# Two raw and three low-part weight tiles, a new product order, spread convolution tiles

## The chip, the cores and the metric

The kernel runs on one core of a Trainium2 chip. The metric is the device time of one execution in microseconds; the value for a kernel is the median of several executions. Five engines take part: PE (TensorE, matrix products), DVE (VectorE, elementwise work), ACT (ScalarE, activations and copies), POOL (GpSimd) and SP, which here issues nearly all transfers from one queue.

## The reference

One decoder layer runs on two groups of tokens with the same weights: a prompt of 512 tokens and 8 samples of 8 tokens, 576 tokens in all, with a model width of 2048.

```python
c = split_columns(rms_norm(x, ln_g) @ w_in)          # 2048 -> 10312 columns
# attention branch: indexer scores, top-k of keys, softmax, times silu(z_attn), @ w_up_attn
u = c['glu_val'] * sigmoid(c['glu_gate'])
dw = depthwise_conv(u_pad, conv_w) + conv_b          # 31 taps, 1024 channels
conv_out = silu(layer_norm(dw, conv_norm_g, conv_norm_b)) @ w_pw + b_pw
branch_conv = (conv_out * silu(c['z_conv'])) @ w_up_conv
merged = sigmoid(c['gate_attn']) * branch_attn + sigmoid(c['gate_conv']) * branch_conv
y = rms_norm(x + merged @ w_out, final_g)
```

Keys, values, indexer keys and the convolution's last rows are outputs too. All is float32.

## The kernel before

**Products.** Activations lie transposed, channels on partitions and the 576 tokens along the free dimension. Each float32 operand is held as two parts in a reduced format (`fp32r`): a high part, and the low part that is left. A product is three matmuls (high by high, high by low, low by high). `weight_unit` (line 140) loads a raw weight tile of 128 x 8 x 128 (512 KB) into a tile called `wraw` (three buffers); `split` (line 147) has ACT write the high part `whi` (line 151, three buffers) and DVE the low part `wlo` (line 153, two buffers). `block` (line 227) runs 48 matmuls on one such unit, for two halves of the tokens.

**Two ways through the input projection.** The first columns (indexer, keys, values, queries, `z_attn`, six of eight convolution tiles and six of eight `z_conv` tiles) go through `block`. The remaining columns (convolution tiles 6 and 7, the last two `z_conv` tiles, 2 x 16 gate tiles) go through `strassen` (line 156): two column tiles, two halves of the channels and two halves of the tokens form a 2 x 2 product of blocks that takes seven products of 24 matmuls instead of eight. I call one call of it a pair; there are 19. A pair loads four raw tiles b11, b12, b22, b21, makes four sums of them on DVE (t3, b12-b11, t2, b21-t2), splits seven tiles, and combines the seven results by seven additions of 128 x 288 on DVE (line 191). In the order before, the products are A11, S1, S2, A12, S3, S4, A22, where S1 to S4 name sums of activation blocks. `XA` (line 943) says where each activation operand lies.

**Sums of activations.** Ahead of the first pair, lines 919 to 933 form S1, S2 and S4 (tiles `s12`, `s4`) through a temporary `f` with one buffer; lines 933 to 939 then overwrite a quarter of the activations with S3. The temporary `f` lies in a pool that is closed before the pool `p3` is opened, which holds the tiles `wx`, `wt` and `sk` of the pairs; `p3` takes its memory.

**Convolution tiles.** `conv_tile` (line 644) multiplies value and gate, then runs 31 taps on DVE (line 706), a small part for the samples (lines 712, 713), and stores the result. Its `u` and `dw` tiles have two buffers each.

**Layer norm of the convolution.** Lines 983 to 1023 run it in two halves of the tokens, eight tiles each, beside the gate pairs. Line 1019 takes a sigmoid on ACT, line 1020 an affine map on DVE.

**End.** `w_pw`, `w_up_attn`, `w_up_conv` go through `block`; then the output projection `w_out` runs in two passes, the second half of the tokens first (line 1107), with one half per pass, so that a raw tile feeds 24 matmuls only. Its residual rows `y` are loaded on the same SP queue (line 1116).

**Order.** A planner lays out each engine's instructions ahead of time, by priority and by its own estimates of durations. Priorities (the function `pri`): weight loads and splits 0, evictions and additions (`EV`) 1, chains such as the sums and the layer norm (`CH`) 3, the convolution's taps and the top-k (`TK`) 5, matmuls 6; the lowest number that is ready goes first. On the chip each engine keeps that order, whatever the real durations are.

Of the kernel before, what the change touches and what calls it, by code (L numbers as in the profile page):

```python
# [20 lines left out]
SEQ = 512  # L21
# [64 lines left out]
def build(tc, I, O):  # L86
# [52 lines left out]

    def weight_unit(w, width, c0, n, kt0, lvl=0):  # L140

        with pri(lvl) if lvl is not None else nullcontext():
            raw = per.tile([128, 8, 128], F32, name="wraw", tag="wraw", bufs=3)
            dma(raw[:, :, :n], ap(w, kt0 * 128 * width + c0, [[width, 128], [128 * width, 8], [1, n]]))
            return split(raw, n)

    def split(raw, n=128):
# [4 lines left out]
        lo = per.tile([128, 8, 128], R, name="wlo", tag="wlo", bufs=2)[:, :k, :n]  # L152
# [3 lines left out]
    def strassen(pool, w, width, ca, cb, A, ev, kts=16, lvl=6, EV=1):  # L156
# [3 lines left out]
        with pri(0):  # L160
            raws = []
            for c0, half, tag in ((ca, 0, "wx"), (cb, 0, "wraw"), (cb, 1, "wraw"), (ca, 1, "wx")):
                t = (per.tile([128, 8, 128], F32, name="wraw", tag="wraw", bufs=3) if tag == "wraw" else
# [3 lines left out]
            b11, b12, b22, b21 = raws  # L167
            t2 = pool.tile([128, 8, 128], F32, name="t2", tag="wt", bufs=2)[:, :n]
            t3 = pool.tile([128, 8, 128], F32, name="t3", tag="wt", bufs=2)[:, :n]

        def bank():
            return ps.tile([128, 512], F32, name="mms", tag="mm", bufs=4)[:, :T2]
# [14 lines left out]
        k1, k5, u2, u3 = (kept() for _ in range(4))  # L187
# [20 lines left out]
        with pri(EV):  # L208
            ev(0, 0, k1)
        p = product(t3, "S3")  # L210
        add(u3, p, u2)
        add(u2, u2, k5)
        add(k5, u3, k5)
        with pri(EV):
            ev(1, 1, k5)
        p = product(b22, "S4")
        add(u2, p, u2)
        with pri(EV):
            ev(0, 1, u2)
        with pri(0):  # L220
            v.tensor_sub(b21, b21, t2)
        p = product(b21, "A22")
        add(u3, p, u3)
        with pri(EV):
            ev(1, 0, u3)
# [418 lines left out]
    def conv_tile(c, pair=None):  # L644
# [17 lines left out]
        else:  # L662
            held = []

            def ev(i, b, x):
                if b == 0:
                    s.activation(sg[:, TS2[i]], x, AF.Sigmoid)
                if (i, b) == (1, 1):
                    held.append(x)
                if (i, b) == (0, 1):  # L670
                    v.tensor_mul(up[:, 30:30 + T2], x, sg[:, :T2])
                if (i, b) == (1, 0):
# [537 lines left out]
```

## Time and profile before

| quantity | value |
|---|---|
| time, median of 3 runs | 1640.47 us (1639.73 to 1640.93) |
| profiled execution: its time, its span | 1639.57 us, 1637.6 us |
| PE busy | 1588.6 us (97%) |
| PE weight loads (PEld) busy | 1538.3 us (94%) |
| DVE busy | 1115.0 us (68%) |
| ACT busy | 664.0 us (41%) |
| POOL busy | 82.1 us (5%) |
| mean granted TensorE clock | 0.991 |
| transfers | 219.53 MB, mean 134 GB/s |

The page also has the busy share of each engine in 40 slices of some 41 us:

```
PE   7999999999999999898999999999999999999997
DVE  6437884476585989999998999667543343445554
PEclk8999999999999999999999999999999999999998
```

A digit is tenths of the slice. PE is full for most of the span; DVE is full from about 640 to 960 us. Neighbouring instructions on DVE overlap in the records, so that the distance from start to start is shorter than the duration.

### The profile page before, as it was taken

How to read it: one execution, taken by the hardware profiler on the slowest of the kernel's cores; microseconds unless marked ns; L12 is line 12 of the kernel's file. 1: busy time of each engine (PE TensorE's matmuls, PEld its weight loads, DVE VectorE, ACT ScalarE, POOL GpSimd, SP SyncE). 2: the span in 40 equal slices, each digit the busy share in tenths (PEclk: the TensorE clock that was granted, in tenths of full speed). 3: DMA queues.
4: the chain of work that ended last, by engine and by line, in shares of the span. 5: the costliest groups of instructions: out<-in, count | busy, mean ns of one | idle time of the engine just before them, and what ended most of it. 6: DMA issues, size and time to landing. Idle time of an engine off the chain costs nothing.

```text
span 1637.6 us, 28579 instructions
## 1 busy us (share of the span) xinstructions
PE 1588.6 (97%) x11594; PEld 1538.3 (94%) x11594; DVE 1115.0 (68%) x1905; ACT 664.0 (41%) x1089; POOL 82.1 (5%) x97
## 2 busy tenths in 40 slices
PE   7999999999999999898999999999999999999997
PEld 5889999999999999888899999999999999899996
DVE  6437884476585989999998999667543343445554
ACT  5434322264555443243344555445421111444443
POOL 4200000001111100000000000000000000400000
PEclk8999999999999999999999999999999999999998
DMA  6732534344444334323345545443744444464864
GB/s 193 203 87 86 163 109 114 99 132 132 136 129 133 93 86 114 112 73 97 102 127 168 149 121 148 133 132 94 242 126 128 127 121 134 142 167 142 258 179 129
DMA packets 318963, 219.53 MB, mean 134 GB/s; under 512 B 14549, under 2 KB 293205, under 8 KB 318112
## 3 DMA queue, kind: packets, MB, share of 16 engines
q1 hardware_dynamic: 316144, 208.27, 43.9%
q0 software_dynamic: 2688, 9.44, 1.8%
q8 instruction: 91, 1.49, 0.4%
q14 instruction: 40, 0.33, 0.1%
HBM read 188.81 MB, written 32.24 MB: 135 GB/s over the span
## 4 chain that ended last, share of the span: by engine, by line
PE 80%; DVE 12%; DMA 3%; issue 2%; ACT 1%; POOL 1%; POOLq 0%; ACTq 0%; DVEq 0%; SPq 0%
PE mm L237 55%; PE mms L181 15%; DVE wlo L153 3%; PE mm L457 2%; DVE dw L706 2%; DMA wraw<-in_w_out 1%; PE po L786 1%; PE po L855 1%; PE pw L768 1%; DVE sk L191 1%; DMA wraw<-in_w_in 1%; POOL ml L1096 1%; PE pw L782 1%; DVE wraw L198 1%; PE pw L517 1%
## 5 line engine op out<-in xcount | busy, mean ns | idle before, releaser
L237 PE MATMUL mm<-x,whi 128*128 128x256 f32 (+2 forms) x2496 | 452.3, 297 | 0.0
L151 ACT CAST whi<-wraw 128x1024 fp32r<-128x1024 f32 (+1 forms) x228 | 238.5, 1046 | 523.0 <-PE mm L237 386.6
L153 DVE TENSOR_TENSOR wlo<-wraw,whi 128x1024 fp32r<-128x1024 f32 (+1 forms) x228 | 279.0, 1224 | 207.4 <-PE mm L237 116.0
L237 PEld LDWEIGHTS mm<-x,whi 128*128 128x128 f32 (+1 forms) x2496 | 377.9, 187 | 5.7 <-issue 3.8
L237 PE MATMUL mm<-x,wlo 128*128 128x256 f32 (+2 forms) x1248 | 274.7, 297 | 0.0
L181 PE MATMUL mms<-x,whi 128*128 128x288 f32 x1216 | 248.2, 298 | 6.8 <-ACT whi L151 5.9
L237 PEld LDWEIGHTS mm<-x,wlo 128*128 128x128 f32 (+1 forms) x1248 | 209.0, 187 | 0.9 <-issue 0.4
L181 PEld LDWEIGHTS mms<-x,whi 128*128 128x128 f32 x1216 | 197.3, 190 | 8.0 <-ACT whi L151 6.6
L181 PE MATMUL mms<-x,wlo 128*128 128x288 f32 x608 | 182.5, 300 | 7.2 <-DVE wlo L153 6.9
L181 PE MATMUL mms<-s,whi 128*128 128x288 f32 x912 | 186.0, 296 | 0.0
L706 DVE SCALAR_TENSOR_TENSOR dw<-u,cp,dw 128x512 f32<-128x512 f32 x240 | 177.8, 750 | 1.6
L181 PEld LDWEIGHTS mms<-s,whi 128*128 128x128 f32 x912 | 146.6, 188 | 0.5 <-ACT whi L151 0.3
L181 PE MATMUL mms<-s,wlo 128*128 128x288 f32 x456 | 135.9, 298 | 6.2 <-DVE wlo L153 6.1
L181 PEld LDWEIGHTS mms<-x,wlo 128*128 128x128 f32 x608 | 115.7, 190 | 10.9 <-DVE wlo L153 10.6
L237 PE MATMUL mm<-mh,wlo 128*128 128x256 f32 (+1 forms) x416 | 122.7, 300 | 3.0 <-DVE wlo L153 3.0
L237 PE MATMUL mm<-mh,whi 128*128 128x256 f32 (+1 forms) x416 | 122.0, 294 | 1.6 <-ACT whi L151 1.6
L237 PE MATMUL mm<-ml,whi 128*128 128x256 f32 (+1 forms) x416 | 121.5, 294 | 0.0
L181 PEld LDWEIGHTS mms<-s,wlo 128*128 128x128 f32 x456 | 85.7, 188 | 9.4 <-DVE wlo L153 9.2
L151 ACT CAST whi<-wx 128x1024 fp32r<-128x1024 f32 x57 | 59.8, 1050 | 82.4 <-PE mms L181 69.5
L237 PE MATMUL mm<-cT,whi 128*128 128x256 f32 (+1 forms) x512 | 88.9, 295 | 0.0
L237 PE MATMUL mm<-aT,whi 128*128 128x256 f32 (+1 forms) x512 | 88.9, 295 | 0.0
L153 DVE TENSOR_TENSOR wlo<-wx,whi 128x1024 fp32r<-128x1024 f32 x57 | 69.6, 1220 | 21.3 <-PE mms L181 18.4
(306 smaller groups left out, 2426.5 us busy)
## 6 DMA issues: line engine op xcount, KB each, us to landing
wraw<-in_w_in SPq DMA_DIRECT2D x122, 512.0 KB
wraw<-in_w_out SPq DMA_DIRECT2D x64, 512.0 KB
wx<-in_w_in SPq DMA_DIRECT2D x38, 512.0 KB
wraw<-in_w_up_attn SPq DMA_DIRECT2D x16, 512.0 KB
wraw<-in_w_up_conv SPq DMA_DIRECT2D x16, 512.0 KB
ga_d<-gt SPq DMA_DIRECT2D x16, 288.0 KB
gc_d<-gt SPq DMA_DIRECT2D x16, 288.0 KB
gc<-gc_d SPq DMA_DIRECT2D x16, 288.0 KB
```

Of the source, the lines that this page charges most:

```text
L151: s.copy(hi, raw[:, :, :n])
L153: v.tensor_sub(lo, raw[:, :, :n], hi.bitcast(F32))
L181: pe.matmul(p, a[:, k], A[x](part, k), start=(k == 0 and j == 0), stop=(k == n - 1 and j == 2))
L191: v.tensor_add(out, a, b)
L198: v.tensor_sub(b12, b12, b11)
L237: pe.matmul(p[h][:n, :HN[h]], a[:, k, :n], x(part, kt, h), start=(kt == 0 and j == 0), stop=(kt == kts - 1 and j == 2))
L457: pe.matmul(p[:, :NQ], a[:, k], xk(part, kt)[:, 128:], start=(kt == 0 and j == 0), stop=(kt == 15 and j == 2))
L517: pe.matmul(d0[:, :W], qdup(part, h)[:, (i - 1) * 128:i * 128], kst[:, :W], start=(part == 0), stop=(part == 1))
L706: v.scalar_tensor_tensor(o1, a1, k1, o1, op0=OP.mult, op1=OP.add)
L768: pe.matmul(S[:, :max(W, 256)], a, x[:, kv, :max(W, 256)], start=(j == 0), stop=(j == 2))
L782: pe.transpose(pt[:, b * 128:(b + 1) * 128], Lt[:, b * 128:(b + 1) * 128], ident)
L786: pe.matmul(out[:, i * 128:(i + 1) * 128], vt[:, b, kv * 128:(kv + 1) * 128], PT[:, b * 128:(b + 1) * 128], start=(b == 0), stop=(b == i))
```

## The change

The raw tiles `wraw` go from three buffers to two and the low parts `wlo` from two to three. From `w_pw` on, a second pair of raw buffers (`wx`, in the pool `p2`) takes every other unit. In `strassen` the two first-needed tiles b11 and b12 now come into `wraw`, the other two, b21 and b22, into `wx`; the sum b12-b11 gets a tile t1 of its own, and b22-b12 is formed in place of b22 after b22's own split. The products run as A11, S1, S2, S4, A12, S3, A22. `s4` gets a pool of its own that is closed with `p3`. The activation sums use four separate rotating tiles for `f`. The `z_conv` pair goes first, convolution tile 6 second and tile 7 fifth among the pairs. The affine map of the layer norm moves from DVE to ACT.

```diff
+    more = []
+    def raw_tile():
+        if more and turn[0] % 2:
+            t = more[0].tile([128, 8, 128], F32, name="wx", tag="wx", bufs=2)
+        else:
+            t = per.tile([128, 8, 128], F32, name="wraw", tag="wraw", bufs=2)
+        turn[0] += 1
+        return t
+    turn = [0]
     def weight_unit(w, width, c0, n, kt0, lvl=0):
-            raw = per.tile([128, 8, 128], F32, name="wraw", tag="wraw", bufs=3)
+            raw = raw_tile()
...
-        lo = per.tile([128, 8, 128], R, name="wlo", tag="wlo", bufs=2)[:, :k, :n]
+        lo = per.tile([128, 8, 128], R, name="wlo", tag="wlo", bufs=3)[:, :k, :n]
...
-            for c0, half, tag in ((ca, 0, "wx"), (cb, 0, "wraw"), (cb, 1, "wraw"), (ca, 1, "wx")):
+            for c0, half, tag in ((ca, 0, "wraw"), (cb, 0, "wraw"), (ca, 1, "wx"), (cb, 1, "wx")):
...
-            b11, b12, b22, b21 = raws
+            b11, b12, b21, b22 = raws
+            t1 = pool.tile([128, 8, 128], F32, name="t1", tag="wt", bufs=2)[:, :n]
             t2 = pool.tile([128, 8, 128], F32, name="t2", tag="wt", bufs=2)[:, :n]
-            t3 = pool.tile([128, 8, 128], F32, name="t3", tag="wt", bufs=2)[:, :n]
...
-            v.tensor_sub(t3, b22, b12)
-            v.tensor_sub(b12, b12, b11)
-        p = product(b12, "S1")
+            v.tensor_sub(t1, b12, b11)
+        p = product(t1, "S1")
...
-            v.tensor_sub(t2, b22, b12)
+            v.tensor_sub(t2, b22, t1)
         p = product(t2, "S2")
         add(u2, p, k1)
+        p = product(b22, "S4")
+        with pri(0):
+            v.tensor_sub(b22, b22, b12)
+        add(v2, u2, k5)
+        add(v2, p, v2)
+        with pri(EV):
+            ev(0, 1, v2)
         p = product(b21, "A12")
-        add(k1, p, k1)
...
+        with pri(0):
+            v.tensor_sub(b21, b21, t2)
+        add(k1, p, k1)
+        with pri(EV):
+            ev(0, 0, k1)
+        p = product(b22, "S3")
+        add(u2, p, u2)
+        add(k5, u2, k5)
+        with pri(EV):
+            ev(1, 1, k5)
         p = product(b21, "A22")
-        add(u3, p, u3)
+        add(u2, p, u2)
...
-            f = p4.tile([128, 4, 2, T2], F32, name="f", tag="f")
+            fs = [p4.tile([128, 2, T2], F32, name="f", tag="f", bufs=4) for _ in range(4)]
...
-    for c in (6, 7):
-        conv_tile(c, lambda ca, cb, ev: strassen(p3, I["w_in"], D_IN, ca, cb, XA, ev))
...
+    order = [("z", j) for j in range(NZ, 8, 2)] + [("a", j) for j in range(0, 16, 2)]
+    order.insert(1, ("c", 6))
+    order.insert(4, ("c", 7))
+    order += [("c0", 0)] + [("g", j) for j in range(0, 16, 2)]
...
-                v.tensor_scalar(x, x, gk, bk, op0=OP.mult, op1=OP.add)
+                s.activation(x, x, AF.Identity, scale=gk, bias=bk)
...
     p3c.__exit__(None, None, None)
+    p7c.__exit__(None, None, None)
...
+    more.append(p2)
```

## Rows read from the trace of the kernel before

**Rows 1.** Windows view by stage: length; busy time (instructions) per engine; clock, DMA, GB/s.
```profile
40.00:640.00 600.00, 600.00 (x4358) 571.00 (x4357) 412.01 (x815) 259.50 (x474) 47.39 (x56) 1.00 0.42 122
684.80:719.85 35.05, 27.36 (x170) 25.21 (x168) 35.03 (x45) 13.48 (x18) 0.00 (x0) 0.90 0.35 95
719.85:893.07 173.22, 162.74 (x1190) 158.42 (x1189) 169.83 (x241) 68.83 (x100) 0.00 (x0) 1.00 0.41 117
893.07:1010.51 117.44, 115.40 (x855) 113.64 (x853) 110.19 (x173) 65.49 (x97) 0.00 (x0) 1.00 0.49 141
1144.70:1400.00 255.30, 255.29 (x1914) 255.03 (x1913) 104.84 (x184) 57.45 (x74) 0.00 (x0) 1.00 0.48 145
1400.00:1440.00 40.00, 35.20 (x232) 33.39 (x231) 20.65 (x32) 19.08 (x40) 18.07 (x16) 1.00 0.61 173
1520.00:1560.00 40.00, 37.33 (x286) 36.28 (x285) 23.68 (x48) 19.46 (x35) 0.00 (x0) 0.96 0.88 269
```

**Rows 2.** Windows view of line 181 (Strassen products): pairs 1, 2-8, 9-13, 16-19.
```profile
684.80:719.85 35.05, 27.19 (x168) 25.21 (x168) 0.90 0.35 95
719.85:893.07 173.22, 162.56 (x1184) 157.80 (x1183) 1.00 0.41 117
893.07:1010.51 117.44, 115.08 (x849) 112.84 (x847) 1.00 0.49 141
1055.53:1144.70 89.17, 87.77 (x660) 87.30 (x658) 1.00 0.38 110
```

**Rows 3.** Waits of PE, 640 to 1200: total us, times, longest.
```profile
PE mms L181 <- DVE wlo L153: 13.0, 22, 2.0
PE mms L181 <- ACT whi L151: 5.9, 3, 4.4
```

**Rows 4.** Timeline of SP: start, length, instruction; start of the Strassen stage.
```profile
684.29 0.99 SPq L165 DMA_DIRECT2D wx<-in_w_in  x2
```

**Rows 5.** Timeline of ACT there; in brackets idle time before, and its releaser.
```profile
688.30 1.04 ACT L151 CAST whi<-wx 128x1024 fp32r<-128x1024 f32 x1 [2.73 <-DMA wx<-in_w_in]
```

**Rows 6.** Timeline of PE, fifth product of the first pair.
```profile
716.08 0.40 PE L181 MATMUL mms<-x,whi 128*128 128x288 f32 x1 [0.58 <-DVE x L917]
```

**Rows 7.** Timeline of DVE, four neighbours in a crowded pair.
```profile
757.53 1.22 DVE L153 TENSOR_TENSOR wlo<-t,whi 128x1024 fp32r<-128x1024 f32 x1
758.67 0.45 DVE L191 TENSOR_TENSOR sk<-mms,sk 128x288 f32<-128x288 f32 x1
759.03 0.74 DVE L706 SCALAR_TENSOR_TENSOR dw<-u,cp,dw 128x512 f32<-128x512 f32 x1
759.69 1.18 DVE L713 TENSOR_REDUCE dw<-tp 128x32 f32<-128x992 f32 x1
```

**Rows 8.** Windows view of line 706 (convolution taps): pairs 4 and 5.
```profile
769.80:797.20 27.40, 10.39 (x15) 1.00 0.35 102
797.20:822.70 25.50, 9.87 (x14) 1.00 0.37 106
```

**Rows 9.** Groups of instructions: line, operation, shapes, count, busy us, mean ns.
```profile
L1020 DVE TENSOR_SCALAR dwl<-dwl,cp 128x288 f32<-128x288 f32 x16 | 6.1, 421 | 0.0
L1019 ACT ACTIVATE lsg<-dwl,cp 128x288 f32<-128x288 f32 x16 | 9.1, 620 | 0.0
```

**Rows 10.** Waits of SP (whole span): issues of weight loads and what they waited for.
```profile
SPq L144 <- DVE wlo L153: 467.0, 113, 16.5
SPq L165 <- DVE sk L191: 224.5, 53, 14.1
```

**Rows 11.** Timeline of SP, output projection, first pass.
```profile
1423.19 0.38 SPq L144 DMA_DIRECT2D wraw<-in_w_out  x1
```

**Rows 12.** Timeline of DVE there.
```profile
1427.11 0.29 DVE L1133 TENSOR_TENSOR y<-y,pw 128x128 f32<-128x128 f32 x1 [6.84 <-DMA y<-in_x_prompt]
```

**Rows 13.** Timeline of ACT there.
```profile
1432.03 1.04 ACT L151 CAST whi<-wraw 128x1024 fp32r<-128x1024 f32 x1 [8.79 <-DMA wraw<-in_w_out]
```

**Rows 14.** Timeline of PE there.
```profile
1428.59 0.42 PE L237 MATMUL mm<-mh,wlo 128*128 128x320 f32 x1 [1.75 <-DVE wlo L153]
```

More of the change, by code (lines that the diff above doesn't have):

```diff
@@ L161, in strassen @@
             raws = []
-            for c0, half, tag in ((ca, 0, "wx"), (cb, 0, "wraw"), (cb, 1, "wraw"), (ca, 1, "wx")):
-                t = (per.tile([128, 8, 128], F32, name="wraw", tag="wraw", bufs=3) if tag == "wraw" else
+            for c0, half, tag in ((ca, 0, "wraw"), (cb, 0, "wraw"), (ca, 1, "wx"), (cb, 1, "wx")):
+                t = (per.tile([128, 8, 128], F32, name="wraw", tag="wraw", bufs=2) if tag == "wraw" else
                      pool.tile([128, 8, 128], F32, name="wx", tag="wx", bufs=2))[:, :n]
@@ L185, in kept @@
             return pool.tile([128, T2], F32, name="sk", tag="sk", bufs=5)
-        k1, k5, u2, u3 = (kept() for _ in range(4))
+        k1, k5, u2, v2 = (kept() for _ in range(4))
         def add(out, a, b):
@@ L209, in strassen @@
             ev(0, 0, k1)
[L210 to L213, printed above, removed]
+        p = product(b22, "S3")
+        add(u2, p, u2)
+        add(k5, u2, k5)
         with pri(EV):
             ev(1, 1, k5)
-        p = product(b22, "S4")
+        p = product(b21, "A22")
         add(u2, p, u2)
         with pri(EV):
[L219 to L222, printed above, removed]
-        add(u3, p, u3)
-        with pri(EV):
-            ev(1, 0, u3)
+            ev(1, 0, u2)
     def block(w, width, c0, x, n=128, kts=16, lvl=6, hs=(0, 1), units=None):
@@ L898, in build @@
     pS = pSc.__enter__()
-    s4 = pS.tile([128, 2, 8, T2], R, name="s4")
+    p7c = tc.tile_pool(name="p7", bufs=1)
+    s4 = p7c.__enter__().tile([128, 2, 8, T2], R, name="s4")
     p4c = tc.tile_pool(name="p4", bufs=1)
@@ L953, in ev @@
             v.tensor_mul(z[b][:, TS2[i]], z[b][:, TS2[i]], x)
-            if (i, b) in ((0, 1), (1, 0)):
+            if i == 1:
                 dma(dst[j + b], z[b])
@@ L963, in ev @@
             s.activation(z[b][:, TS2[i]], x, AF.Sigmoid)
-            if (i, b) in ((0, 1), (1, 0)):
+            if i == 1:
                 dma(dst[j + b], z[b])
         strassen(p3, I["w_in"], D_IN, c0 + 128 * j, c0 + 128 * (j + 1), XA, ev)
-    for c in (6, 7):
-        conv_tile(c, lambda ca, cb, ev: strassen(p3, I["w_in"], D_IN, ca, cb, XA, ev))
-    for j in range(NZ, 8, 2):
-        silu_pair(C_ZC, zc_d, j)
-    for c0, dst in ((C_GA, ga_d), (C_GC, gc_d)):
-        for j in range(0, 16, 2):
-            gate_pair(c0, dst, j)
-        if c0 == C_GA:
+    order = [("z", j) for j in range(NZ, 8, 2)] + [("a", j) for j in range(0, 16, 2)]
+    order.insert(1, ("c", 6))
+    order.insert(4, ("c", 7))
+    order += [("c0", 0)] + [("g", j) for j in range(0, 16, 2)]
+    for kind, j in order:
+        if kind == "c":
+            conv_tile(j, lambda ca, cb, ev: strassen(p3, I["w_in"], D_IN, ca, cb, XA, ev))
+        elif kind == "z":
+            silu_pair(C_ZC, zc_d, j)
+        elif kind == "a":
+            gate_pair(C_GA, ga_d, j)
+        elif kind == "g":
+            gate_pair(C_GC, gc_d, j)
+        else:
             pBc.__exit__(None, None, None)
```

42 lines of the change are left out of this document (20 added, 22 removed).

## The prediction

> **What bounds the kernel now.** I read the windows view by stage first, since a share over the whole span hides where PE stands still. The reader is to see there [rows 1] that PE is busy in all 600 us from 40 to 640 and in all but 0.01 us of the 255 us from 1144.7 to 1400. Nothing but fewer matmuls could shorten those stretches, and the change removes no matmul. Holes lie in the Strassen stage (684.8 to 1144.7) and in the output projection. The busy share understates them, so I take the length of a pair instead: the last four pairs take 89.17 us [rows 2], 22.3 us each, and nothing disturbs them. Against that pace the first pair, counted from the end of the block before it, takes 35.05 us (12.75 too long), the next seven 173.22 us (156.1 at the pace, 17.1 too long) and the next five 117.44 us (111.5, 5.9 too long) [rows 2]. That is 35.8 us. In the output projection PE idles 4.8 us of the 40 after 1400 and 2.7 us of the 40 after 1520, and the granted clock there is 0.96, worth another 1.6 us [rows 1]: 9.1 us. What the change can win at most is therefore about 45 us of 1640.
>
> Next the waits of PE: nearly all in the Strassen stage are for the low parts (13.0 us in 22 waits, never over 2.0) and for high parts (5.9 us, of which one wait has 4.4) [rows 3]. Behind them stands DVE, busy 35.03 of 35.05 us in the first pair and 169.8 of 173.2 in the next seven [rows 1]. So PE waits for an engine that is full, and the question is how much of DVE's work can stand later.
>
> **What a pair costs DVE.** From start to start a 128x1024 operation takes 1.14 us, an addition of 128x288 0.36 us and a tap 0.66 us [rows 7]. A gate pair has four sums, seven splits and seven additions: 11 x 1.14 + 7 x 0.36 = 15.1 us, which leaves 7.2 us of the 22.3. Pairs 4 and 5 carry 15 and 14 taps [rows 8], 15.1 + 15 x 0.66 = 25.0 us before anything else, so PE follows DVE there. The planner fills what it takes for gaps of DVE with taps; the chip's DVE is slower than that, by 25.0 - 22.3 = 2.7 us in such a pair. A paired convolution tile needs 31 x 0.66 us plus four sample operations of 1.1 us [rows 7] and small ones, about 26 us.
>
> **The change part by part.**
>
> *New order of products and the tiles b11, b12.* Operations are equal in number: four sums, seven splits, seven additions before and after. What moves is the first pair. Its b11 comes into `wx`, whose memory the temporary of the sums holds, so the loads are issued only at 684.29 [rows 4] and the high part starts at 688.30 [rows 5], 4.0 us later; PE stands for 4.4 us [rows 3] and then runs at a clock of 0.90 over the pair [rows 1], worth 3.5 us of 35. With b11 and b12 in `wraw`, which the pairs before don't hold, both should be there early. The wait then moves to b22, needed for t2 two products (6.3 us) later: landing at about 688.5, then 1.14 for t2 and 1.0 for the high part [rows 5], gives 690.7 against a need at 684.8 + 6.3 = 691.1. But the pair ends later on something else: a matmul of S3 starts only at 716.08, released by DVE's overwriting of the activations [rows 6], and DVE is full until then. S3 is now sixth instead of fifth, so one product more (22.3/7 = 3.2 us) can stand ahead of that point. The gain is bounded by 1 us (DVE as late as now, the hole only moves) and 12.75; I take 6, nearer to the DVE bound.
>
> *Three low parts, two raw tiles.* The slots between load and use stay five, so a load that waits for a free raw tile (467.0 us of waiting of SP on `wlo`, 224.5 at the pairs' loads [rows 10]) is issued at about the same moment: the low part goes one slot earlier, and frees its raw tile one slot earlier. What is new is that DVE may be one product, 3.2 us, further behind before PE feels it, while no wait for a low part is over 2.0 us [rows 3]. A convolution tile's overdraft is 2.7 us in each of some 2.3 pairs, 6 us, of which one lead of 3.2 us is absorbed if the lead is full when the tile starts. For the 600 us before, the cost lies between 0 and 6 us (three loads late by 2 us while the first transfers crowd the queue): PE is full there now, and 48 matmuls take some 6.4 us against a pair of loads in flight of about 4.0 us [rows 4, 5] plus 2.2 us of splitting each. I take 0.
>
> *Tiles spread.* Tile 6 goes from first to second, tile 7 from second to fifth. DVE's work is the same, but between the two there are now gate pairs with 7.2 us to spare each, in which the lead is refilled. The end of the layer norm moves later by a few pairs; after it six pairs are undisturbed now, which is the cover, and if that cover goes, the sums for `w_pw` come late. For pairs 2 to 8, with the extra lead: gain between -3 (more crowding in one place) and 17.1. Two tiles at 6 - 3.2 = 2.8 each, and some 2.5 of ragged order, leave 8; I take a gain of 9.
>
> *Rotating temporaries.* Four tiles of the same total size; they take away a wait of the next quarter for the last copy of the one before, on an engine that is full anyway: 0, from 0 to 2 inside the first pair's bounds.
>
> *Affine map on ACT.* Sixteen operations leave DVE (6.1 us) and come to ACT, priced by the neighbour with the same operands at 0.62 us, 9.9 us [rows 9]. ACT is busy 65.5 of 117.4 us there and DVE 110.2 [rows 1], so it fits. With the extra lead, of 5.9 us I take 2.5 (from -1 to 5.9); waits that follow the chain of the layer norm remain.
>
> ScalarE against VectorE is the one rule I weigh. The row says that the map is dearer on ACT, 0.62 against 0.42 us [rows 9]. The Trainium skill ("ScalarE: Activation LUTs", Rules for kernel authors) says to put multiplications and additions on VectorE; by it the move would cost 16 x 0.2 = 3 us, by the row of DVE's load it gives back up to 6. I go by the load.
>
> *Output projection.* A raw tile feeds 24 matmuls there, about 3 us, so loads are the tight part. In the first pass a load issued at 1423.19 [rows 11] is used only at 1432.03, ACT having stood for 8.79 us [rows 13]; DVE meanwhile stood 6.84 us on a row of y [rows 12] with a low part behind it, which gave PE its wait of 1.75 us [rows 14]. Two more raw tiles are two units, 6 us, of loads ahead, and a third low part takes the second kind. Of 9.1 us I take 5.5; the bounds are 0 (y and the loads still queue in one order) and 9.1.
>
> The pool of s4 costs nothing: its tile is last read at the fourth product of the last pair, some 9 us before `w_pw` needs what takes its place.
>
> **Sum.** 6 + 9 + 2.5 + 5.5 = 23 us. The profiled execution took 1639.57 us (span 1637.6), so 1616.6 by its own time; the median of the runs is 0.9 us higher, so 1617.
>
> **Rivals.**
>
> 1. *DVE's total decides.* The planner fills taps as greedily as before, wherever the tiles stand; leads are eaten in the first pair, which hands its arrears on. For it: DVE is full for 205 of 208 us [rows 1]. Against it: six later pairs have 7.2 us to spare each. Then pairs 1 to 13 give 1 + 2 + 1, and the output projection 5.5: 9.5 us, 1631.
>
> 2. *The change does not do what it says.* The planner orders everything anew from its own estimates, and new waits eat the gain: an order that holds additions back, the first transfers late by the 6 us above, the output projection unchanged because y still stands ahead of the loads. Then the 9.5 of rival 1 without 5.5, less some 4: 1640.
>
> 3. *Slower: b22 late in every pair.* b21 and b22 now both lie in `wx`; b21 is freed by the seventh product's split, and b22, if SP issues them in the written order, stands behind it, though t2 needs it at the third product. Against it: from that split, at worst one product ahead of its matmuls, to t2 there are about 3.2 + 3.2 + 6.3 - 2.2 = 10.5 us, and the loads landed in 4.0 us [rows 4, 5]. For it: beside other traffic one took 8.8 us [rows 11, 13]. From 10.5 us on it decides; at 12.5 us each of 18 pairs pays 2 us, 36, and with 15 of the other gains left the time is 1640 + 36 - 15 = 1661.
>
> **How the numbers follow.** Forecast 0.64, rival 1 0.23, rival 2 0.06, rival 3 0.07. Less than 0.2% (3.3 us) can't be told from no change by a measurement of this kernel. The forecast's own bounds added up are wide; I take its middle, 1604 to 1626. Rival 1 reaches up to 1635. So the range is 1604 to 1635. Faster: the forecast, nearly all of rival 1: 0.87. Within 0.2%: most of rival 2: 0.05. Slower: rival 3 and a little of rival 2: 0.08.
>
> **What would show it.** Right: the first Strassen matmul starts within 0.3 us of the block before it, the clock of that stretch is near 1.00, and pair 1 lasts about 29 us; pairs 2 to 8 last about 164 us together; waits of PE for low parts in the stage fall from 13.0 to under 6; in the output projection PE idles under 3.5 us. Rival 1 shows as a full DVE with pairs of 24 to 27 us still there; rival 2 as holes in places that have none now, before 640 most of all; rival 3 as waits of ACT's high part for t2, and of t2 for a transfer, in most pairs. Wrong altogether would be a gain of over 40 us, since the holes don't hold that much, or a loss before 640.

## The result, and the profile after

The changed kernel takes 1615.38 us (median of 4 runs, 1615.24 to 1615.72) against 1640.10 us for the kernel before in the same session (4 runs, 1638.72 to 1640.93). The ratio is 0.985, 95% interval 0.9833 to 0.9867: about 25 us faster, far outside the 0.2% that a measurement can't tell. The forecast was 1617. The profiled execution took 1615.24 us, its span is 1613.2.

The page of the changed kernel: busy time of the engines, the 40 slices of DVE, and the shares of the chain that ended last; the last line is that chain in the kernel before.

```profile
PE 1577.7 (98%) x11594; PEld 1535.1 (95%) x11594; DVE 1107.6 (69%) x1889; ACT 668.8 (41%) x1105; POOL 79.4 (5%) x97
DVE  5436985385765888999999899977543333455554
PE 89%; DVE 5%; DMA 2%; issue 2%; POOL 1%; ACT 0%; SPq 0%; POOLq 0%; ACTq 0%; DVEq 0%
PE 80%; DVE 12%; DMA 3%; issue 2%; ACT 1%; POOL 1%; POOLq 0%; ACTq 0%; DVEq 0%; SPq 0%
```

The number of matmuls is unchanged. In the chain that ended last, PE's share rose from 80% to 89% and DVE's fell from 12% to 5%: PE is held up by DVE less often. What that is worth, the stages show.

The windows view by stage, which answers to [rows 1] and [rows 2]: the block stage, pair 1, pairs 2 to 8, pairs 9 to 13, the later block stage, and two stretches of the output projection (columns as in [rows 1]). The pairs are cut here at the first of their 168 matmuls. [rows 1] cuts them up to 1.5 us later, so the last two lines give pairs 2 to 8 and 9 to 13 of the kernel before by the same count.

```profile
40.00:640.00 600.00, 600.00 (x4356) 569.75 (x4355) 406.90 (x812) 260.47 (x474) 44.86 (x56) 1.00 0.41 120
686.96:720.14 33.18, 26.33 (x170) 25.16 (x169) 32.64 (x43) 12.07 (x18) 0.00 (x0) 0.90 0.41 108
720.14:881.07 160.93, 157.82 (x1182) 156.63 (x1181) 155.48 (x208) 66.00 (x92) 0.00 (x0) 1.00 0.41 117
881.07:993.46 112.39, 112.39 (x846) 112.17 (x845) 102.83 (x150) 61.44 (x94) 0.00 (x0) 1.00 0.51 151
1128.70:1386.00 257.30, 255.94 (x1918) 255.47 (x1917) 106.55 (x182) 57.99 (x73) 0.00 (x0) 1.00 0.50 150
1386.00:1426.00 40.00, 39.35 (x269) 38.65 (x268) 22.60 (x37) 21.91 (x45) 17.92 (x16) 1.00 0.63 179
1506.00:1546.00 40.00, 40.00 (x337) 40.00 (x336) 25.63 (x47) 20.02 (x33) 0.00 (x0) 1.00 0.95 274
```

```profile
719.98:892.40 172.42, 161.94 (x1184) 157.62 (x1183) 169.06 (x239) 68.55 (x99) 0.00 (x0) 1.00 0.41 116
892.40:1009.05 116.65, 114.61 (x849) 112.85 (x847) 109.73 (x174) 64.72 (x96) 0.00 (x0) 1.00 0.49 139
```

The reader is to see three things. Pairs 2 to 8 are 11.5 us shorter and DVE is no longer full there (155.5 of 160.9, before 169.1 of 172.4). Pairs 9 to 13 have no hole left (PE is busy in all of the 112.39 us), though DVE had slack there before as well. Pair 1 is hardly shorter, and its clock is as low as before.

PE's waits between 640 and 1200, which answer to [rows 3]:

```profile
PE mms L191 <- DVE wlo L166: 5.8, 5, 2.9
PE mms L191 <- ACT whi L164: 3.6, 3, 2.4
```

From 22 waits for low parts there are five left.

The lengths of the stages, found by counting the 168 matmuls of each pair in the trace of each profiled execution, give one table for the whole study (us; "start" is everything up to the end of the last block before the pairs; pair 1 is counted from there, every other pair from its first matmul; "blocks" are `w_pw`, `w_up_attn` and `w_up_conv`; the last column is the output projection with its tail):

| run | span | start | pair 1 | 2-8 | 9-13 | 14-19 | blocks | output |
|---|---|---|---|---|---|---|---|---|
| before | 1637.6 | 685.0 | 35.0 | 172.4 | 116.6 | 134.6 | 255.8 | 238.0 |
| after | 1613.2 | 687.0 | 33.2 | 160.9 | 112.4 | 135.3 | 257.3 | 227.1 |
| e1 no late raw tiles | 1635.2 | 685.3 | 33.2 | 160.8 | 112.4 | 135.3 | 255.5 | 252.8 |
| e2 tiles not spread | 1622.5 | 685.4 | 33.2 | 168.9 | 113.4 | 136.4 | 257.9 | 227.4 |
| e3 two raw, two low | 1637.8 | 689.0 | 33.1 | 166.1 | 117.8 | 140.2 | 260.4 | 231.2 |
| e4 old products | 1623.0 | 687.2 | 31.0 | 168.2 | 114.3 | 136.9 | 257.9 | 227.6 |
| e5 two raw, three low alone | 1660.9 | 686.2 | 36.9 | 178.7 | 116.3 | 134.3 | 255.5 | 253.1 |
| e6 first units apart | 1615.4 | 689.1 | 33.6 | 160.0 | 112.4 | 135.3 | 257.9 | 227.2 |
| e7 sums' tiles elsewhere | 1627.9 | 685.4 | 50.7 | 159.4 | 112.4 | 135.3 | 257.1 | 227.6 |
| e8 affine map on DVE | 1611.4 | 684.6 | 33.2 | 160.9 | 112.4 | 136.0 | 257.0 | 227.3 |
| e9 loads and t1 early | 1612.6 | 686.8 | 29.6 | 161.6 | 112.4 | 136.3 | 258.3 | 227.4 |
| e10 three raw, two low | 1632.7 | 684.1 | 31.6 | 169.1 | 118.2 | 140.1 | 259.8 | 229.9 |
| e11 late raw tiles alone | 1636.4 | 685.1 | 36.5 | 172.4 | 116.6 | 134.6 | 260.0 | 231.2 |
| e12 spread alone | 1634.8 | 683.8 | 36.6 | 161.9 | 117.9 | 137.3 | 259.6 | 237.7 |

So the span's 24.4 us come from pairs 2 to 8 (11.5), the output projection (11.0), pairs 9 to 13 (4.3) and pair 1 (1.8), less 2.0 of the start, 0.7 of pairs 14 to 19 and 1.5 of the blocks. The start varies between 684.6 and 687.0 among after, e1, e2, e8 and e9, which all open alike. Differences of some 2 us in it, and of 1 us elsewhere, carry no argument here.

**Pair 1.** The timeline of the changed kernel, engines PE, ACT, SP and DVE; these lines answer to [rows 4] to [rows 6]:

```profile
686.96 0.43 PE L191 MATMUL mms<-x,whi 128*128 128x288 f32 x2
692.67 0.53 PE L191 MATMUL mms<-s,whi 128*128 128x288 f32 x2 [2.39 <-ACT whi L164]
696.06 0.61 PE L191 MATMUL mms<-s,wlo 128*128 128x288 f32 x1 [2.86 <-DVE wlo L166]
687.61 0.68 ACT L928 CAST s<-f 128x576 fp32r<-128x576 f32 x1
688.32 0.76 DVE L929 TENSOR_TENSOR s<-f,s 128x576 fp32r<-128x576 f32 x1
689.21 1.01 SPq L178 DMA_DIRECT2D wx<-in_w_in  x2
690.32 1.22 DVE L207 TENSOR_TENSOR t<-wraw 128x1024 f32<-128x1024 f32 x1
```

The first matmul follows the block without a gap, where the kernel before stood 4.4 us. Three microseconds later the second product has nothing to work on: its operand is the sum b12-b11 in the new tile t1 (line 207). That tile lies in `p3`, the pool that takes the memory of `f`, so it can't be written before the last reads of `f` are done: ACT's copy at 687.61 and DVE's low part at 688.32, which ends at 689.08. DVE comes to t1 at 690.32. The first loads into `wx` lie in that memory too and are issued at 689.21, 4.9 us later than in [rows 4]; 2.0 of these are the later start of the stage.

**Pairs 4 and 5.** The windows of the taps alone (line 717 now) answer to [rows 8]:

```profile
766.30:788.60 22.30, 7.24 (x10) 1.00 0.51 148
788.60:810.87 22.27, 6.34 (x10) 1.00 0.41 119
```

Ten taps each instead of 15 and 14 (a window also counts a tap that only reaches into it: 14 and 14 start in those two pairs before, ten and nine now). No pair from 2 on has more than ten, and these two run at the undisturbed pace of 22.3. The longest of pairs 2 to 8 is now pair 6 with 24.7 us.

**Affine map.** The group that answers to [rows 9]:

```profile
L1038 ACT ACTIVATE dwl<-dwl,cp 128x288 f32<-128x288 f32 x16 | 9.6, 623 | 0.0
```

The price of the new operation was right: 623 ns, and 620 was assumed.

**Weight loads and output projection.** SP's waits over the span answer to [rows 10] (the fifth line is one more of the kernel before), the timeline below them to [rows 12] to [rows 14]:

```profile
SPq L157 <- DVE wlo L166: 441.1, 123, 18.2
SPq L178 <- DVE sk L201: 50.6, 17, 7.5
SPq L178 <- DVE wx L217: 77.6, 14, 15.0
SPq L178 <- DVE wlo L166: 69.2, 24, 6.6
```

```profile
SPq L165 <- DVE wlo L153: 80.9, 13, 14.5
```

```profile
1420.49 1.05 ACT L164 CAST whi<-wraw 128x1024 fp32r<-128x1024 f32 x1 [7.16 <-DMA wraw<-in_w_out]
1413.51 0.48 DVE L1153 TENSOR_TENSOR y<-y,pw 128x128 f32<-128x128 f32 x2 [6.10 <-DMA y<-in_x_prompt]
1397.57 0.56 PE L248 MATMUL mm<-me,whi 128*128 128x320 f32 x2 [0.38 <-ACT whi L164]
```

The pairs' loads wait 50.6 us for additions instead of 224.5, but 77.6 us for sums formed in `wx` take part of their place: with the waits for low parts it is 197.4 us in these lines against 305.4. ACT still stands 7.2 us for a load and DVE 6.1 us for a row of y, nearly as long as before. But PE notices neither: 0.38 us is its longest wait for a weight in this stage. That more units are split ahead is the likely reason.

### The profile page after: what moved, and what is told of

Same layout as the page of the kernel before. It is cut to its first block, busy times and chain, and to the rows that moved or that the text cites. A ratio compares the mean times of both kernels' runs of the same rounds, so it can differ in the third digit from the quotient of the medians.

```text
span 1613.2 us, 28357 instructions
## 1 busy us (share of the span) xinstructions
PE 1577.7 (98%) x11594; PEld 1535.1 (95%) x11594; DVE 1107.6 (69%) x1889; ACT 668.8 (41%) x1105; POOL 79.4 (5%) x97
## 4 chain that ended last, share of the span: by engine, by line
PE 89%; DVE 5%; DMA 2%; issue 2%; POOL 1%; ACT 0%; SPq 0%; POOLq 0%; ACTq 0%; DVEq 0%
PE mm L248 57%; PE mms L191 21%; PE mm L468 2%; DVE wlo L166 2%; PE po L797 1%; PE po L866 1%; PE pw L779 1%; POOL ml L1116 1%; DVE dw L717 1%; PE pw L793 1%; DMA y<-in_x_sample 1%; PE pw L528 1%; PE pw L1149 0%; DMA wx<-in_w_in 0%; DMA xt<-in_x_prompt 0%
## 5 line engine op out<-in xcount | busy, mean ns | idle before, releaser
L164 ACT CAST whi<-wraw 128x1024 fp32r<-128x1024 f32 (+1 forms) x157 | 163.8, 1044 | 360.3 <-PE mm L248 282.2
L166 DVE TENSOR_TENSOR wlo<-wraw,whi 128x1024 fp32r<-128x1024 f32 (+1 forms) x157 | 191.3, 1219 | 119.1 <-ACT whi L164 118.4
L191 PE MATMUL mms<-x,whi 128*128 128x288 f32 x1216 | 241.8, 295 | 1.6 <-ACT whi L164 1.3
L164 ACT CAST whi<-wx 128x1024 fp32r<-128x1024 f32 x128 | 134.2, 1049 | 232.9 <-PE mm L248 119.1
L166 DVE TENSOR_TENSOR wlo<-wx,whi 128x1024 fp32r<-128x1024 f32 x128 | 156.9, 1226 | 68.0 <-ACT whi L164 66.3
L191 PE MATMUL mms<-x,wlo 128*128 128x288 f32 x608 | 177.8, 296 | 2.3 <-DVE wlo L166 2.3
L191 PE MATMUL mms<-s,wlo 128*128 128x288 f32 x456 | 135.3, 299 | 3.6 <-DVE wlo L166 3.5
```

The lines of the kernel that those rows point to most:

```text
L164: s.copy(hi, raw[:, :, :n])
L166: v.tensor_sub(lo, raw[:, :, :n], hi.bitcast(F32))
L191: pe.matmul(p, a[:, k], A[x](part, k), start=(k == 0 and j == 0), stop=(k == n - 1 and j == 2))
```

## The experiments

All were timed beside the kernel before. Its median was 1639.1 to 1639.3 us in these three groups of runs.

### e1: without the late raw tiles

```diff
-    more.append(p2)
```

> The changed kernel, but without the second pair of raw tiles from w_pw on: two raw tiles to the end. Theory (the late raw tiles carry the output projection): the output projection, 227.1 us after and 238.1 us before, goes back to 236 to 242 us, the Strassen stage stays as it is, the time is 1625 to 1630 us. Rival (the third low part carries it, as DVE no longer stands on a row of y with a low part behind it): the output projection stays under 231 us, the time under 1619 us.

Measured: 1638.40 us, ratio 0.9997 (0.9987 to 1.0007). The output projection takes 252.8 us, 25.7 more than in the changed kernel; the pairs are unchanged. ACT's waits for transfers after 1385, and PE's longest hole:

```profile
ACT whi L164 <- DMA wraw<-in_w_out: 74.1, 29, 10.7
1417.30 0.63 PE L248 MATMUL mm<-mh,whi 128*128 128x320 f32 x1 [8.39 <-ACT whi L164]
1382.00:1422.00 40.00, 30.86 (x197) 29.83 (x196) 17.46 (x30) 16.72 (x36) 16.98 (x16) 0.88 0.51 146
```

The theory was right in its place and too small in size. With only two raw tiles this stage is worse than with the three of the kernel before, so the late tiles first repay what the swap costs here (some 15 us) and then bring 11. Around the hole the granted clock is lower (0.88 over the 40 us), which lengthens what PE then does.

### e2: convolution tiles back at the front

```diff
-    order = [("z", j) for j in range(NZ, 8, 2)] + [("a", j) for j in range(0, 16, 2)]
-    order.insert(1, ("c", 6))
-    order.insert(4, ("c", 7))
+    order = [("c", 6), ("c", 7)] + [("z", j) for j in range(NZ, 8, 2)] + [("a", j) for j in range(0, 16, 2)]
```

> The changed kernel, but with convolution tiles 6 and 7 as the first two pairs again. Theory (the lead of a third low part and the spread share the gain in pairs 2 to 8, 162.0 us after, 173.2 before): pairs 2 to 8 take 166 to 169 us, the time is 1619 to 1622 us. Rival A (the spread is all of it): 172 to 174 us and 1625 to 1627 us. Rival B (the spread is nothing): 161 to 163 us and 1614 to 1616 us.

Measured: 1625.29 us, ratio 0.9915 (0.9898 to 0.9931). Pairs 2 to 8 take 168.9 us, 8.0 more than after and 3.5 less than before. So the gain is shared, as the theory has it, at the upper end of its range, with a time in the range of rival A. Their window:

```profile
718.58:887.52 168.94, 160.64 (x1183) 157.09 (x1181) 166.64 (x228) 65.83 (x92) 0.00 (x0) 1.00 0.42 120
```

DVE is full again (166.6 of 168.9). Spreading, given the rest of the change, is worth 8.0 of the 11.5 us of this stage.

### e3: two low parts

```diff
-        lo = per.tile([128, 8, 128], R, name="wlo", tag="wlo", bufs=3)[:, :k, :n]
+        lo = per.tile([128, 8, 128], R, name="wlo", tag="wlo", bufs=2)[:, :k, :n]
```

> The changed kernel, but with two low-part tiles, so four slots between load and use instead of five. Theory (the third low part is the lead that hides DVE's arrears): pairs 2 to 13, 274.9 us after and 290.7 us before, go back by 8 us or more, to over 283 us, and the time is 1624 to 1635 us. Rival (the spread and the order of products do it, DVE's lead does not matter): pairs 2 to 13 under 278 us, the time 1615 to 1618 us.

Measured: 1639.52 us, ratio 1.0000 (0.9991 to 1.0010). The loss of 24 us lies in every stage but pair 1, most in pairs 2 to 19 (5.2, 5.4 and 4.9). The theory held for pairs 2 to 13 (283.9 us), and the time is 4.5 us beyond its range. But one slot is missing in all here, so the split itself isn't tested; e10 does that.

### e4: old order of products, with two raw and three low-part tiles

```diff
-            for c0, half, tag in ((ca, 0, "wraw"), (cb, 0, "wraw"), (ca, 1, "wx"), (cb, 1, "wx")):
+            for c0, half, tag in ((ca, 0, "wx"), (cb, 0, "wraw"), (cb, 1, "wraw"), (ca, 1, "wx")):
...
-            v.tensor_sub(t1, b12, b11)
-        p = product(t1, "S1")
+            v.tensor_sub(t3, b22, b12)
+            v.tensor_sub(b12, b12, b11)
+        p = product(b12, "S1")
```

> The changed kernel, but with the Strassen pair of before: its loads (b11 and b21 in wx, b12 and b22 in wraw), its sums and its order of products. Theory (the order matters for the first pair alone, where the wait moved from the first product to the third): pair 1 with the wait ahead of it 33 to 37 us against 33.2, pairs 2 to 13 within 3 us of 274.9, the time 1614 to 1619 us. Rival (the order of products frees raw tiles and results earlier and carries pairs 2 to 8): pairs 2 to 8 at 168 us or more, the time 1622 us or more.

Measured: 1624.53 us, ratio 0.9909 (0.9892 to 0.9925). The rival held: the order, with the places of the tiles, is worth 9 us, and none of it in pair 1, which is even 2.2 us shorter with the old one. Pairs 2 to 8 lose 7.2 us, 6.2 of it in pair 7 alone (29.4 us against 23.2), pairs 9 to 13 lose 1.9 and pairs 14 to 19 lose 1.6. The largest holes of PE, in pair 7:

```profile
839.64 0.53 PE L194 MATMUL mms<-s,whi 128*128 128x288 f32 x2 [1.70 <-ACT whi L164]
842.33 0.85 PE L194 MATMUL mms<-s,whi 128*128 128x288 f32 x2 [2.16 <-ACT whi L164]
```

PE waits for high parts here, and ACT for the sums of raw tiles that they are made from. In the old order these need b22 at the second product, and b22 comes into one of only two `wraw` tiles. That this is what makes the sums late isn't shown: DVE has no gap between 828 and 846 us either. Behind the holes the granted clock is lower, 0.88 over the pair.

### e5: the kernel before with two raw and three low-part tiles alone

```diff
-            raw = per.tile([128, 8, 128], F32, name="wraw", tag="wraw", bufs=3)
+            raw = per.tile([128, 8, 128], F32, name="wraw", tag="wraw", bufs=2)
...
-        lo = per.tile([128, 8, 128], R, name="wlo", tag="wlo", bufs=2)[:, :k, :n]
+        lo = per.tile([128, 8, 128], R, name="wlo", tag="wlo", bufs=3)[:, :k, :n]
```

> The kernel before with two raw and three low-part tiles and nothing else. Theory (a third low part for a third raw tile is what hides DVE's arrears, whatever the order): the Strassen stage, 458.8 us before and 441.8 after, falls to 452 us or less, while the output projection with two raw tiles goes to about 252 us as in the kernel without the late raw tiles; time 1643 to 1649 us. Rival (the old order of products, whose b12 and b22 both lie in these tiles, needs three of them): Strassen stage 458 us or more, time 1652 us or more.

Measured: 1661.38 us, ratio 1.0136 (1.0115 to 1.0156). Alone, the swap costs 22 us, and the Strassen stage takes 466.2 us: the rival held. All of PE's waits between 680 and 1160 are of one kind:

```profile
PE mms L181 <- ACT whi L151: 27.0, 10, 10.4
```

No wait for a low part is left, which is what a third one is for. The missing raw tile takes back more, in the first eight pairs (8.2 us) and in the output projection (15.1).

### e6: first units in raw tiles of their own

```diff
-        units = [weight_unit(I["w_in"], D_IN, C_KI, 72, u, lvl=None) for u in (0, 8)]
+        units = []
+        for u in (0, 8):
+            raw = p0.tile([128, 8, 72], F32, name="wki", tag="wki", bufs=2)
...
+            units.append(split(raw, 72))
```

> The changed kernel, with the two small first weight units (72 columns) in raw tiles of their own in the opening's pool, so that both raw tiles are free for the next columns. Theory (the 2.2 us that the changed kernel is late at the Strassen stage's start come from the third load, which waits for a raw tile): the block before the Strassen stage ends at 684.5 to 685.3 us instead of 687.0, the time is 1612.5 to 1614 us. Rival (the opening is late by its planned order): end at 686.5 us or later, time 1615 us or more.

Measured: 1614.09 us, ratio 0.9845 (0.9825 to 0.9866), not to be told from the changed kernel's 0.985. The start isn't shorter (689.1), so the theory fell: the 2.0 us there are not the missing raw tile.

### e7: temporaries of the sums in the row tiles, p3 opened early

```diff
-    p4c = tc.tile_pool(name="p4", bufs=1)
-    p4 = p4c.__enter__()
+    p3c = tc.tile_pool(name="p3", bufs=1)
+    p3 = p3c.__enter__()
...
-            fs = [p4.tile([128, 2, T2], F32, name="f", tag="f", bufs=4) for _ in range(4)]
+            fs = [st("f").rearrange("p (k t) -> p k t", k=2) for _ in range(3)]
+            fs.append(fs[0])
```

> The changed kernel, with the temporaries of the activation sums in the kernel's three rotating row tiles instead of a pool of their own, so that the pairs' pool takes no memory from them and its tiles are free before the first pair. Theory (the first pair's holes come from tiles of the pairs that wait for the temporaries' memory): its first three products run without a wait over 0.5 us, the pair takes 27 to 30 us with the wait ahead of it instead of 33.3, the time is 1609 to 1612 us. Rival (DVE is full until S3's operands are there, whatever comes free earlier): the hole moves to S3, the pair takes 32 to 34 us, the time is 1614 to 1616 us.

Measured: 1630.40 us, ratio 0.9948 (0.9931 to 0.9965). Pair 1 takes 50.7 us, at a granted clock of 0.73. PE's waits between 684 and 740:

```profile
PE mms L191 <- ACT s L928: 7.4, 8, 2.4
PE mms L191 <- DVE s L929: 3.5, 6, 1.6
```

It waits for the sums, which now share three tiles with the `z_conv` rows and come late. Neither theory nor rival had this, and the run doesn't test whether the shared memory holds the weights up; e9 does.

### e8: affine map back on DVE

```diff
-                s.activation(x, x, AF.Identity, scale=gk, bias=bk)
+                v.tensor_scalar(x, x, gk, bk, op0=OP.mult, op1=OP.add)
```

> The changed kernel with the affine map of the layer norm on DVE again. Theory (6 us of work off a full DVE; a third low part covers most of the rest): pairs 9 to 13 take 114 to 116 us instead of 112.9, the time is 1616 to 1618 us. Rival (the lead covers it all): pairs 9 to 13 within 0.5 us of 112.9, the time 1615 to 1616 us.

Measured: 1615.51 us, ratio 0.9861 (0.9840 to 0.9882); pairs 9 to 13 take 112.4 us, as after. The rival held: in the changed kernel DVE has the slack for these 16 operations.

### e9: first weight loads and t1 out of f's memory

```diff
+    pEc = tc.tile_pool(name="pE", bufs=1)
+    early.append(pEc.__enter__())
...
-                      pool.tile([128, 8, 128], F32, name="wx", tag="wx", bufs=2))[:, :n]
+                      early[0].tile([128, 8, 128], F32, name="wx", tag="wx", bufs=2))[:, :n]
...
-            t1 = pool.tile([128, 8, 128], F32, name="t1", tag="wt", bufs=2)[:, :n]
+            t1 = early[0].tile([128, 8, 128], F32, name="t1", tag="t1", bufs=1)[:, :n]
```

> The changed kernel with the two raw tiles of the weights and the tile t1 in a pool that is opened ahead of the last block's temporaries f, so that the first weight loads and the first t1 no longer lie in the memory that f gives up; t2 and the three row tiles stay where they were. Theory (pair 1 loses its second product because the first loads and t1 wait for f's last copy): the holes of 2.4 and 2.9 us ahead of the second product's matmuls go, pair 1 takes 27 to 30 us instead of 33.3, pairs 2 to 8 stay at 162, and the time is 1609 to 1613 against 1615.4 for the changed kernel. Rival (VectorE is full in pair 1, so the work that comes earlier only moves the hole to the sums or to the low parts): pair 1 31.5 to 34 us, time 1614 to 1617.

Measured: 1614.59 us (5 runs, 1612.59 to 1618.11), ratio 0.9851 (0.9835 to 0.9866). The windows of pair 1 and of pairs 2 to 8, and the first hole of PE with DVE's work ahead of it:

```profile
686.80:716.43 29.63, 25.04 (x171) 23.75 (x170) 29.63 (x41) 12.13 (x17) 0.00 (x0) 0.94 0.23 64
716.43:878.06 161.63, 158.41 (x1182) 156.69 (x1181) 157.74 (x211) 65.72 (x93) 0.00 (x0) 1.00 0.42 117
```

```profile
674.47 1.22 DVE L207 TENSOR_TENSOR t<-wraw 128x1024 f32<-128x1024 f32 x1
693.35 1.22 DVE L212 TENSOR_TENSOR t<-wx,t 128x1024 f32<-128x1024 f32 x1
695.69 0.53 PE L191 MATMUL mms<-s,whi 128*128 128x288 f32 x2 [2.38 <-ACT whi L164]
```

t1 is there 16 us earlier, and the second product follows the first at once. The hole stands one product later, where t2 comes late while DVE is busy in all 29.63 us. Pair 1 is 3.6 us shorter, as the theory has it, of which the stages behind it give some 3 back in pieces of about 1 us; the time as a whole isn't distinguishable from the changed kernel's, as the rival has it. Both are right in part: f's memory set the first hole, and behind it DVE sets the pair.

### e10: three raw and two low-part tiles, the rest of the change kept

```diff
-            t = per.tile([128, 8, 128], F32, name="wraw", tag="wraw", bufs=2)
+            t = per.tile([128, 8, 128], F32, name="wraw", tag="wraw", bufs=3)
...
-        lo = per.tile([128, 8, 128], R, name="wlo", tag="wlo", bufs=3)[:, :k, :n]
+        lo = per.tile([128, 8, 128], R, name="wlo", tag="wlo", bufs=2)[:, :k, :n]
```

> The changed kernel with three raw tiles and two low-part tiles, the split of the kernel before, and everything else of the change: five slots, as after, so that only the split differs. Theory (the third low part gives the sequence its lead): pairs 2 to 13 take 281 us or more, against 275 in the changed kernel, and the time is 1622 or more. Rival (only the number of slots counts, and the loss of the run with two raw and two low tiles came from its four slots): pairs 2 to 13 take 275 us, the time is 1614 to 1617.

Measured: 1634.79 us, ratio 0.9974 (0.9963 to 0.9984); pairs 2 to 13 take 287.2 us against 273.3. With five slots as in the changed kernel the split alone decides 19 us, so the theory holds. DVE's largest wait between 684 and 1140, in this kernel, in the changed kernel and in the kernel before:

```profile
DVE wlo L166 <- PE mms L191: 25.7, 27, 2.0
```

```profile
DVE wlo L166 <- ACT whi L164: 19.8, 25, 2.1
```

```profile
DVE wlo L153 <- PE mms L181: 30.9, 31, 2.0
```

With two low parts, DVE comes to a split while PE is still reading the low part whose place it needs, and stands for 25.7 us in 27 waits with everything else of its queue behind it. With three, no split waits for PE; the splits wait for the high part, which is the work itself. Of the 30.9 us before, 29.4 lie after 893, where DVE wasn't full: so it is not only DVE's load that the third low part covers, but DVE's standing still.

### e11: the kernel before with the late raw tiles alone

```diff
+            if more and turn[0] % 2:
+                raw = more[0].tile([128, 8, 128], F32, name="wx", tag="wx", bufs=2)
...
+    more.append(p2)
```

> The kernel before with one edit: the two raw tiles of the later stages in a pool of their own, as the change has them, which the output projection keeps. Three raw and two low-part tiles, the old order of products and of convolution tiles. Theory (those tiles carry the whole gain of the output projection): that stage takes 227 to 230 us instead of 238.1, the stages before it are as before, time 1628 to 1631. Rival (the third low part is needed as well): the stage takes 233 us or more, time 1634 or more.

Measured: 1635.52 us, ratio 0.9978 (0.9969 to 0.9987). The output projection takes 231.2 us, between theory and rival; the time is in the rival's range. Two waits of PE:

```profile
PE mm L243 <- ACT whi L157: 2.3, 1, 2.3
PE mm L243 <- DVE wlo L159: 2.6, 4, 1.7
```

The first is a new hole at the start of `w_pw`, where the blocks lose 4.1 us and so give most of it away again in this execution, with 1638.45 us the longest of the ten (the last section has the clock behind it); the second stands in the output projection. So the late tiles alone bring 6.8 of this stage's 11.0 us. For the other 4.1 the third low part is needed: without it e3 takes 231.2 us as well, with all the rest of the change.

### e12: the kernel before with the spread tiles alone

```diff
-    for c in (6, 7):
-        conv_tile(c, lambda ca, cb, ev: strassen(p3, I["w_in"], D_IN, ca, cb, XA, ev))
...
+    for kind, c in (("z", NZ), ("c", 6), ("a", 0), ("a", 2), ("c", 7)):
```

> The kernel before with one edit: the paired convolution tiles in the changed kernel's spread order. Theory (the spread takes work from VectorE in the pairs where it is full, whatever the products' order): pairs 2 to 8 take 165 to 168 us instead of 173.2, time 1631 to 1635. Rival (the old order's waits for the next product's high part stand in the way all the same): pairs 2 to 8 take 172 to 174 us, time 1638 to 1641.

Measured: 1633.73 us, ratio 0.9962 (0.9950 to 0.9974). Pairs 2 to 8 take 161.9 us, better than the theory said and 1 us more than after. But of these 10.5 us, 7.7 are lost again behind them in this profiled execution: 1.3, 2.6 and 3.8 us in the next three stages. (It took 1636.79 us, the longest of the six; by the medians 5.5 us are left.) One place of the loss, pair 10:

```profile
905.95:931.95 26.00, 24.06 (x170) 23.82 (x169) 19.11 (x29) 9.82 (x15) 0.00 (x0) 0.93 0.60 173
```

```profile
916.81 0.46 DVE L998 TENSOR_TENSOR acc<-dwl 128x288 f32<-128x288 f32 x1 [3.10 <-DMA dwl<-dw_d]
919.96 0.40 PE L181 MATMUL mms<-x,wlo 128*128 128x288 f32 x1 [1.94 <-DVE wlo L153]
921.28 0.68 PE L181 MATMUL mms<-x,whi 128*128 128x288 f32 x2
```

DVE, far from full, stands 3.10 us for a row of the layer norm; the split behind it is late, PE stands 1.94 us, and then runs for a while at the lower clock (0.68 us for two matmuls; 0.42 is the length at the upper one).

### The parts together

| part | alone, on the kernel before | taken out of the changed kernel |
|---|---|---|
| two raw, three low | +22.1 (e5) | +19.4 (e10) |
| late raw tiles | -3.7 (e11) | +23.0 (e1) |
| spread tiles | -5.5 (e12) | +9.9 (e2) |
| order and places of products | not run | +9.2 (e4) |
| affine map | not run | +0.1 (e8) |

Differences of medians in us, the left column against the kernel before beside it, the right against 1615.4 (other runs of the kernel before moved by 1 us between the groups). The three that ran alone add up to +13 us; together with the new order they make -25. The swap is bad by itself; what it costs in the output projection the late raw tiles repay (e1), what it costs in pairs 2 to 8 is of the size that the order gives there (e4), and the third low part then pays in every stage but pair 1 (e3). The order alone on the kernel before was not run.

## Why the prediction was right, and where it was not

**First pair: mis-sized, 1.8 for 6 us.** "Both should be there early" was right for b11: the first matmul had no gap. The failed step is "the wait then moves to b22". I didn't see that t1 itself, a new tile, lies in the memory of `f`, nor that the `wx` loads would be issued at 689.21. The wait moved one product, not two, and the clock stayed at 0.90. e9 shows the cause. With that put right the pair takes 29.6 us (29 was said), with DVE busy throughout, as the argument on S3 had it. PE waits no longer for DVE's overwriting in S3, but for parts of its weights: at most 0.62 us in the changed kernel, 1.29 us in e9.

**Three low parts, two raw tiles: right in effect, incomplete in cause.** I argued that a lead of one product absorbs DVE's overdraft. e10 shows the lead at work, but also waits of DVE itself for PE, which I hadn't read in the trace of before: 29.4 us after 893. They explain why pairs 9 to 13, where the kernel before has no tap left, gained 4.3 instead of 2.5 (with two low parts these pairs take 118.2 us in e10 and 117.8 in e3). That is all there was to gain: the excess was 4.3 and not 5.9, since two of these pairs carry the layer norm's own matmuls and take 22.8 us with PE busy throughout. The same waits fit that e3, e10 and e12 are longer in pairs 14 to 19 (140.2, 140.1 and 137.3 us against 135.3): there the third low part does what I expected of the cover ("six pairs are undisturbed"). "Issued at about the same moment" held only together with the rest of the change; e5 shows a loss of 22 us without it. The 0 for the 600 us before held.

**New order: right sum, wrong place.** I said that operations are equal in number and that what moves is the first pair. e4 shows the reverse: pair 1 loses 2.2 by it, the pairs after it gain 10.7. I take it that the order decides how long each of the few raw tiles is held; no run isolates that.

**Tiles spread: right, 11.5 for 9.** At most ten taps to a pair, DVE below full, pairs from 22.3 to 24.7: the overdraft of DVE was the cause (with the 14 taps that start in each of pairs 4 and 5, 2.0 us by the prediction's prices and not 2.7). e12 alone reaches 161.9, e2 loses 8.0. The pace of 22.3 that all this is measured by was right by luck: its window holds 660 of the 672 matmuls of four pairs and 1 us of the next block; counted by matmuls, three of the four take 22.30 and the last 23.1.

**Rotating temporaries: not isolated.** e7, which changed their place, moved other things with them.

**Affine map: 0 for a share of 2.5.** The price was right, the gain nil (e8). The Trainium skill ("ScalarE: Activation LUTs", Rules for kernel authors) says to put multiplications and additions on VectorE. By [rows 9] the move to ACT would cost 3 us if it were on the path; the runs show no difference either way.

**Output projection: mis-sized, 11.0 for 5.5, and past the bound of 9.1.** The mechanism held (e1, e11, e10). The bound was wrong because I took it from PE's idle time, after having said that the busy share understates what is lost. By pace it reads otherwise: a column tile of the first pass now takes 118.9 / 16 = 7.4 us and of the second 95.8 / 16 = 6.0; before, the passes took 124.1 and 101.4, and at the undisturbed pace of 7.37 and 5.98 the excess was 11.9 us. The Trainium skill ("Perfetto Trace Analysis", Identifying the Most-Contended Engine) says that matmul busy time is not a good measure of the headroom and names the busy share of the weight loads beside the matmul work done per time. The trace agrees on the weight loads: in the two windows of [rows 1] the weight loads leave 6.6 + 3.7 = 10.3 us idle, where the matmuls leave 7.5.

**The sum.** 23 was said, 24.4 measured in the spans, with errors of +2.5, +1.8 and +5.5 in three terms, -4.2 in that of the first pair and -4.2 in the stages put at nothing. That it came out so near is luck. The total is better than its terms.

**Rivals.** DVE's total didn't decide: the work is the same but for the affine map, and pairs 4 and 5 run at pace. Of a new order of the plan little shows: the stages put at nothing lost 4.2 us, for which no run gives the cause. b22 is late at times, as the third rival has it: the sum t2 waits for its transfer 7.9 us in all, eight times, but never over 2.2 us. So the 10.5 us that I estimated as reserve weren't always enough for DVE, but PE hardly felt it: its waits for high parts are 3.6 us in the stage, 2.4 of them for t1 in pair 1.

## What to carry to other kernels

A ring of buffers between an engine that fills and an engine that reads stalls both: look for waits of the filling engine for the reader, since an engine that stands there holds up everything queued behind it, even where its busy share is low. Price an edit against the undisturbed pace of a stage, not against idle rows, and ask of each new tile whose memory it takes and when that is given up. Parts of one change can cost alone what they earn together: test them both ways, alone and taken out.

## What the runs showed that was not expected

A hole of some 2 us of PE can cost more than itself, since the lower of the two clock levels comes behind it. The windows that begin at the hole at the start of `w_pw`, of 2.33 us in e11 and of 1.89 us in e9:

```profile
1153.60:1170.00 16.40, 16.05 (x108) 15.70 (x109) 10.24 (x15) 7.91 (x13) 0.00 (x0) 0.90 1.06 349
```

```profile
1134.70:1150.00 15.30, 14.78 (x109) 14.55 (x110) 10.82 (x16) 7.57 (x11) 0.00 (x0) 1.00 1.04 331
```

In e11 the clock is 0.90 over the next 16.4 us, in e9 it stays at 1.00. The hole of 1.86 us at the same place in e10 has 0.88 behind it over 14.2 us, that of 2.10 in e12 has 0.91 over 18.0, and this is part of why the blocks take 259.6 to 260.0 us in these three runs. In e12's pair 10, 1.94 us of standing came with 0.93 over 26.0 us, 3.7 us above the pace; in the changed kernel's first pair two holes of 2.39 and 2.86 came with 0.90 over 33.3 us. The lengths of these windows differ, but each of the four single holes comes with nearly the same loss: 0.10 x 16.4, 0.12 x 14.2, 0.09 x 18.0 and 0.07 x 26.0 make 1.6 to 1.8 us of full clock. Why 1.89 us in e9 was spared and 1.86 in e10 wasn't stays open; in pair 4 a hole of 1.96 us is followed by 1.00 over 15 us in the kernel before and by 0.89 in e11. There the lower clock cost nothing: the pair takes 27.42 us in both, since DVE is full.

The swap of one raw tile for one low part, at the same number of slots, moves the time by 22 us up in the kernel before (e5) or 19 us down with the rest of the change (e10), of which the order of seven products and two buffers that are used only at the end are the largest parts (e4, e1).
